# A layer's diagonal state recurrence, from 64 serial complex steps to real scans in a turning frame

## The chip, the cores and the metric

One core of one Trainium2 chip runs the whole program as a single launch. Times are device microseconds of that core, from executions of the compiled kernel; the profile is one execution, recorded by the hardware profiler. Engines are named as in the profile: PE (matmul), DVE (vector), ACT (scalar), POOL (GpSimd), SP (which issues most loads).

## The reference, cut to what matters

The program is one step of a two-layer hybrid encoder. The change touches the S5 branch of layer 0: 32 groups (G) of 64 complex states, each driven by 16 channels.

```python
mag = jnp.exp(lam_re * dt)
ab_re = mag * jnp.cos(lam_im * dt)
ab_im = mag * jnp.sin(lam_im * dt)
...
bu_re = jnp.einsum('btgc,gpc->btgp', ug, bb_re)
bu_im = jnp.einsum('btgc,gpc->btgp', ug, bb_im)
...
_, _, h_re, h_im = lax.associative_scan(_cplx_combine, (a_re, a_im, bu_re, bu_im), axis=1)
y = (jnp.einsum('btgp,gcp->btgc', h_re, c_re) - jnp.einsum('btgp,gcp->btgc', h_im, c_im))
...
y = jax.nn.gelu(y)
y = y * jax.nn.sigmoid(y @ w_glu + b_glu)
```

So h[t] = a·h[t−1] + bu[t] with one complex a per group and state, over a prompt of 16 meta and 2048 frames, and over eight streams of 16 frames.

## The kernel before, in words

Matmuls are made of three products (`mm3`, L111 to L113): operands are split in a high and a low part ("h" and "l": `split`, L105 casts the high part on ACT, L106 subtracts on DVE or POOL).

Every engine runs its instructions in the order of its queue. A planner of the tile framework sets that order when the program is built, by its own estimate of times, within the dependences and the reuse of memory; a tile that takes over another's memory waits until that one's last reader is done. Pools on the "right" side stack on each other.

`phase_in0` normalizes the frames in six blocks (`norm`, `seq`) and multiplies each by the first 1024 columns of the input weights (tiles pm0). The results for the S5 branch stay in `uas` until the end, when ACT copies them out in 32 transfers to `d_ua` (L291). Between the blocks come steps for later phases: at i == 1 `s5_open` (L555) computes the S5 coefficients in many small DVE operations, from λ and dt to the powers of a (`pw`, 17 of them), a16 and bp. At i == 4 the first weight tile of layer 0 is loaded and split ahead: wfh by ACT, wfl by DVE.

`phase_l0` then runs the tiles of the remaining input projection through `mtile`: three passes ("thirds") over pairs of blocks, PE tiles `pm`, a causal convolution on DVE (L537, L539), an ACT SiLU (L408) and the gate matmul L414 (`pg`) that takes its result. After every tile from the third on, `next(s5g, None)` (L496) lets the generator `s5` put out one more step. Its steps are:
- for q in 0..7, four groups each: load u (`s5_u`), the input coefficients `ba` on DVE (L690 to L694), transposes, and the matmul that gives each chunk of 16 frames its contribution, written to `ee` (129 columns a group, two halves: real parts on partitions 0 to 63, imaginary on 64 to 127);
- the scan over chunks: `advance` merges the columns by two (L751 to L755, one operation on POOL), then 64 steps of five DVE operations over all 32 groups (L764 to L768) go along the even columns, and `advance` fills in the odd ones;
- for q in 0..7 the y part: coefficients `ca` (one product on POOL, L818) and matmuls that give y, stored to `d_ys`;
- the end ("s5g"): 32 loads of y (L867) into the place that the y part's pools had, GELU on ACT (L878), and the gated product on PE.

Of the kernel before, what the change touches and what calls it, by code (L numbers as in the profile page):

```python
# [9 lines left out]
F32 = mybir.dt.float32  # L10
# [9 lines left out]
NSEQ = 8  # L20
# [17 lines left out]
def P(e, name, bufs=1, side=None):  # L38
    return e.tc.tile_pool(name=name, bufs=bufs, side=side, reuse_waits="tile")
# [163 lines left out]
def phase_in0(e):  # L203
# [6 lines left out]
    with P(e, "a_w") as wp, P(e, "a_sb", 2) as sb, PS(e, "a_ps") as ps:  # L210
# [37 lines left out]
        for i, bi in enumerate(seq):  # L248
# [306 lines left out]
def s5_open(e, ps):  # L555
# [4 lines left out]
    kb = opn(e, "s5kb", side="right")  # L560
    with P(e, "s5prm", side="right") as sb:
# [37 lines left out]
        pw = s5.pw = keep.tile([128, 2, G, 17], F32, name="s5pw")  # L599
# [4 lines left out]
        t1 = sb.tile([128, G, 16], F32, name="s5t1")  # L604
        t2 = sb.tile([128, G, 16], F32, name="s5t2")
        k = 1
        while k < 16:
# [48 lines left out]
        for q in range(2):  # L656
            hr = sb.tile([128, 128], F32, name=f"s5hr{q}")
            for j, nm in enumerate(("re", "im")):
                src = e.i["state_s5_" + nm].rearrange("a s g p -> (a s g) p")[128 * q:128 * (q + 1)]
                nc.sync.dma_start(hr[:, 64 * j:64 * (j + 1)], src)  # L660
            nc.tensor.transpose(ph[:, q, :], hr, e.ident)
        for q in range(2):
            v.tensor_copy(s5.h0.rearrange("p g (q s) -> p q s g", q=2)[:, q],
                          ph.rearrange("p q (s g) -> p q s g", s=4)[:, q])

# [10 lines left out]
def s5(e, ps):  # L676
# [6 lines left out]
    with P(e, "s5a", side="right") as sb:  # L683
        for q in range(8):
            gs = slice(4 * q, 4 * q + 4)
            ur = s5_u(e, sb, q)
# [8 lines left out]
            v.tensor_copy(p.bb[:, gs, :], ba[:, :, 15, :])  # L695
            bat = sb.tile([128, 4, 2, 128], F32, name="s5bat")
# [17 lines left out]
        v.memset(ee[:, :, 0:1], 0.0)  # L714

        st = sb.tile([128, G, NSEQ], F32, name="s5st")
        s2 = sb.tile([128, G, NSEQ], F32, name="s5s2")
# [5 lines left out]
        sg = sb.tile([128, NSEQ, G], F32, name="s5sg")  # L723
# [9 lines left out]
        yield  # L733

        a32 = sb.tile([128, 2, G], F32, name="s5a32")
        a1 = sb.tile([128, G], F32, name="s5c1", bufs=2)
        a2 = sb.tile([128, G], F32, name="s5c2", bufs=2)
        v.tensor_mul(a1, p.a16[:, 0], p.a16[:, 0])
        v.tensor_mul(a2, p.a16[:, 1], p.a16[:, 1])
        v.tensor_sub(a32[:, 0], a1, a2)  # L740
        v.scalar_tensor_tensor(a32[:, 1], p.a16[:, 0], 2.0, p.a16[:, 1], op0=OP.mult, op1=OP.mult)

        def advance(dst, src, n, g0):

            gs = slice(g0, g0 + G // 2)
            h = ee[:, gs, src:src + 2 * n - 1:2]
            d = ee[:, gs, dst:dst + 2 * n - 1:2]
            t1 = sb.tile([128, G // 2, n], F32, name="s5ba")
            t2 = sb.tile([128, G // 2, n], F32, name="s5tm")
            bc = lambda j, ph: p.a16[ph, j, gs, None].to_broadcast([h[ph].shape[0], G // 2, n])  # L750
            v.tensor_tensor(t2[UP], h[LO], bc(1, LO), op=OP.mult)  # L751
            v.tensor_tensor(t2[LO], h[UP], bc(1, UP), op=OP.mult)
            nc.gpsimd.tensor_tensor(t1, h, bc(0, slice(0, 128)), op=OP.mult)
            v.tensor_add(d, d, t2)
            v.tensor_add(d, d, t1)  # L755

        for g0 in (0, G // 2):
            advance(2, 1, PCH // 2, g0)
            yield
        for c in range(2, PCH + 1, 2):  # L760
            a1 = sb.tile([128, G], F32, name="s5c1", bufs=2)
            a2 = sb.tile([128, G], F32, name="s5c2", bufs=2)
            h = ee[:, :, c - 2]
            v.tensor_tensor(a2[UP], h[LO], a32[LO, 1], op=OP.mult)  # L764
            v.tensor_tensor(a2[LO], h[UP], a32[UP, 1], op=OP.mult)
            v.tensor_tensor(a1, h, a32[:, 0], op=OP.mult)
            v.tensor_add(a2, a2, ee[:, :, c])
            v.tensor_add(ee[:, :, c], a1, a2)  # L768
            if c % 32 == 0:
                yield  # L770
        for g0 in (0, G // 2):
            advance(1, 0, PCH // 2 + 1, g0)
            yield
# [9 lines left out]
    cls(e, "s5kb")  # L783
    with P(e, "s5y", side="right") as sb:

        pw = p.pw
        cp = sb.tile([128, 2, G, 17], F32, name="s5cp")
        v.tensor_copy(cp[UP, 0], pw[UP, 0])
        v.tensor_scalar(cp[LO, 0], pw[LO, 1], -1.0, None, op0=OP.mult)
        v.tensor_scalar(cp[UP, 1], pw[UP, 1], -1.0, None, op0=OP.mult)  # L790
        v.tensor_scalar(cp[LO, 1], pw[LO, 0], -1.0, None, op0=OP.mult)
        cc = [sb.tile([128, G, 16], F32, name=f"s5c{j}") for j in range(2)]
        for j, nm in enumerate(("re", "im")):
            cr = sb.tile([128, 4, 2, 64], F32, name="s5tm2")
# [15 lines left out]
        for q in range(8):  # L810
            gs = slice(4 * q, 4 * q + 4)
            ur = s5_u(e, sb, q)
# [3 lines left out]
            v.tensor_tensor(ca, cp[:, 0, gs, :, None].to_broadcast(sh), cc[0][:, gs, None, :].to_broadcast(sh),  # L816
                            op=OP.mult)
            nc.gpsimd.tensor_tensor(tmp, cp[:, 1, gs, :, None].to_broadcast(sh), cc[1][:, gs, None, :].to_broadcast(sh),  # L818
                                    op=OP.mult)
# [12 lines left out]
            for k in range(8):  # L832
                nc.sync.dma_start(tz[16 * k:16 * (k + 1)],
                                  e.kp[q].rearrange("(g c) a b -> c g a b", g=4)[:16, :, 7 - k:23 - k, :])
            for mh in range(2):
# [18 lines left out]
    cls(e, "s5ee", "s5keep")  # L854
# [1201 lines left out]
```

## Time and profile before

| | before |
|---|---|
| median of 3 runs | 3155.74 us (3153.85 to 3159.35) |
| profiled execution, its span | 3151.14 us, 3149.4 us |
| mean granted TensorE clock | 0.98 |
| PE busy | 3002.9 us (95%), 17435 matmuls |
| weight loads (PEld) busy | 2717.0 us (86%) |
| DVE busy | 1728.6 us (55%) |
| ACT, POOL busy | 1056.1 us (34%), 904.6 us (29%) |
| chain that ended last | PE 59%, DVE 8%, DMA 2% |

A share is an average over all stages. Busy PE is not PE at its full clock: the granted clock stands beside it in the views by stretch. A row of the timeline gives start, duration, engine, line, operation and tiles; in brackets stands the idle time before it and what ended it. "ACTq" and "SPq" rows are the issue of transfers by these engines. A view by groups puts the instructions of one line and shape together: count, busy time, mean nanoseconds, idle time before them.

### The profile page before, as it was taken

The page shows a single profiled execution, that of the slowest core. Times are in us where ns is not written, and L with a number is a line of the kernel's source. Part 1 is how long each engine was busy: PE and PEld are TensorE (multiplying, and loading weights), DVE is VectorE, ACT ScalarE, POOL GpSimd, SP SyncE. Part 2 cuts the span into 40 slices and gives each one's busy share as a digit, 9 for nine tenths or more (in the row PEclk, how much of TensorE's full clock was granted, in tenths as well). Part 3 has the DMA queues.
Part 4 walks back from the last instruction along what each step waited for, and adds up shares of the span by engine and source line. Part 5 has one row for each costly group of instructions (what it writes and reads, how often), then busy time and mean ns, then how long its engine had stood idle before and what let it go on. Part 6 is the DMA issues. An engine that isn't in the chain of part 4 may idle for free.

```text
span 3149.4 us, 45106 instructions
## 1 busy us (share of the span) xinstructions
PE 3002.9 (95%) x17435; PEld 2717.0 (86%) x17435; DVE 1728.6 (55%) x3449; ACT 1056.1 (34%) x1858; POOL 904.6 (29%) x931
## 2 busy tenths in 40 slices
PE   8999978997999998999999999999999999999999
PEld 8999877996987887766799999999998897888887
DVE  4236798464447886243355667766620026665664
ACT  4223332335334443211224555555531112211211
POOL 6104424443225663111202111111110014433432
PEclk9999989998999999999999999999999999999999
DMA  6437433559454556755532111111122158444442
GB/s 213 117 82 206 125 117 113 159 166 177 141 159 125 157 156 183 232 185 172 158 132 73 51 51 50 49 50 49 49 81 75 55 151 251 140 119 133 136 124 74
DMA packets 444034, 396.36 MB, mean 126 GB/s; under 512 B 43401, under 2 KB 392785, under 8 KB 443818
## 3 DMA queue, kind: packets, MB, share of 16 engines
q1 hardware_dynamic: 333164, 268.13, 29.9%
q10 hardware_dynamic: 110654, 125.33, 12.0%
q8 instruction: 137, 2.24, 0.3%
q14 instruction: 79, 0.65, 0.1%
HBM read 262.12 MB, written 131.27 MB: 125 GB/s over the span
## 4 chain that ended last, share of the span: by engine, by line
PE 59%; DVE 8%; DMA 2%; issue 1%; ACT 1%; POOL 0%; SPq 0%; DVEq 0%; POOLq 0%; ACTq 0%
PE p_pm L112 8%; PE p_pm L113 8%; PE p_pm L111 8%; PE r_pm L112 4%; PE r_pm L113 4%; PE r_pm L111 4%; PE pa L111 3%; PE pa L112 3%; PE pa L113 3%; DVE p_d L1639 1%; PE pn L1288 1%; PE pc L1291 1%; DVE p_xc L537 1%; PE pa L1156 1%; DVE m_qs L1131 1%
## 5 line engine op out<-in xcount | busy, mean ns | idle before, releaser
L111 PE MATMUL p_pm<-pu,p_wh 128*128 128x384 f32 (+1 forms) x1568 | 512.2, 327 | 0.2 <-ACT pu L105 0.2
L112 PE MATMUL p_pm<-pu,p_wh 128*128 128x384 f32 (+1 forms) x1568 | 511.9, 327 | 0.0
L113 PE MATMUL p_pm<-pu,p_wl 128*128 128x384 f32 (+1 forms) x1568 | 511.3, 326 | 0.0
L111 PE MATMUL pm<-ub,wh 128*128 128x384 f32 (+1 forms) x1136 | 381.4, 336 | 3.4 <-ACT wh L105 2.9
L112 PE MATMUL pm<-ub,wh 128*128 128x384 f32 (+1 forms) x1136 | 380.1, 335 | 1.6 <-DVE ub L106 1.6
L113 PE MATMUL pm<-ub,wl 128*128 128x384 f32 (+1 forms) x1136 | 376.1, 334 | 0.0
L111 PEld LDWEIGHTS p_pm<-pu,p_wh 128*128 128x128 f32 x1568 | 294.2, 188 | 1.8 <-issue 1.2
L112 PEld LDWEIGHTS p_pm<-pu,p_wh 128*128 128x128 f32 x1568 | 294.6, 188 | 1.0 <-issue 0.8
L113 PEld LDWEIGHTS p_pm<-pu,p_wl 128*128 128x128 f32 x1568 | 294.5, 188 | 0.0
L111 PEld LDWEIGHTS pm<-ub,wh 128*128 128x128 f32 x1136 | 218.6, 193 | 9.0 <-issue 4.3
L112 PEld LDWEIGHTS pm<-ub,wh 128*128 128x128 f32 x1136 | 218.7, 193 | 3.0 <-DVE ub L106 2.1
L112 PE MATMUL r_pm<-rol,r_gh 128*128 128x512 f32 x544 | 217.6, 400 | 3.8 <-POOL rol L106 3.6
L113 PEld LDWEIGHTS pm<-ub,wl 128*128 128x128 f32 x1136 | 218.1, 192 | 1.2 <-issue 1.1
L111 PE MATMUL r_pm<-roh,r_gh 128*128 128x512 f32 x544 | 217.5, 400 | 0.9 <-ACT p_o L1549 0.9
L113 PE MATMUL r_pm<-roh,r_gl 128*128 128x512 f32 x544 | 216.9, 400 | 0.9 <-DVE r_gl L106 0.9
L106 POOL TENSOR_TENSOR p_wl<-p_wr,p_wh 128x1024 fp32r<-128x1024 f32 x34 | 81.8, 2407 | 385.3 <-ACT p_wh L105 372.9
L106 POOL TENSOR_TENSOR wl<-wr,wh 128x1024 fp32r<-128x1024 f32 x47 | 119.2, 2537 | 243.1 <-ACT wh L105 236.8
L112 PEld LDWEIGHTS r_pm<-rol,r_gh 128*128 128x128 f32 x544 | 102.7, 189 | 24.3 <-POOL rol L106 4.1
L113 PEld LDWEIGHTS r_pm<-roh,r_gl 128*128 128x128 f32 x544 | 102.8, 189 | 22.6 <-DVE r_gl L106 1.3
L111 PEld LDWEIGHTS r_pm<-roh,r_gh 128*128 128x128 f32 x544 | 102.3, 188 | 21.9 <-ACT p_o L1549 1.3
L106 POOL TENSOR_TENSOR p_xcl<-p_xc,p_xch 128x384 fp32r<-128x384 f32 (+1 forms) x48 | 46.8, 975 | 245.9 <-ACT p_xch L105 209.3
L1639 DVE RECIPROCAL p_d<-p_d 128x384 f32<-128x384 f32 (+1 forms) x48 | 116.7, 2430 | 0.6
(715 smaller groups left out, 6810.9 us busy)
## 6 DMA issues: line engine op xcount, KB each, us to landing
wr<-in_ev_w_in_dram SPq DMA_DIRECT2D x47, 512.0 KB
p_wr<-in_od_w_in_dram SPq DMA_DIRECT2D x40, 512.0 KB
d_in<-p_o ACTq DMA_DIRECT2D x80, 192.0 KB
m_rw<-d_grow SPq DMA_DIRECT2D x18, 512.0 KB
s5u<-d_ua SPq DMA_DIRECT2D x32, 274.0 KB
d_v<-vo ACTq DMA_DIRECT2D x68, 128.0 KB
m_va<-d_v SPq DMA_DIRECT2D x17, 512.0 KB
d_h<-o_x ACTq DMA_DIRECT2D x17, 512.0 KB
```

The source lines that it names most:

```text
L106: (nc.gpsimd if pool else nc.vector).tensor_tensor(l, x, h, op=OP.subtract)
L111: nc.tensor.matmul(out, a[0], b[0], start=start, stop=False, **kw)
L112: nc.tensor.matmul(out, a[0], b[1], start=False, stop=False, **kw)
L113: nc.tensor.matmul(out, a[1], b[0], start=False, stop=stop, **kw)
L537: v.tensor_scalar(out, x(3), pc[:, m, cw + 3:cw + 4], pc[:, m, cb:cb + 1], op0=OP.mult, op1=OP.add)
L1131: v.tensor_tensor(qs[:, 4 * j:4 * j + 4, :n].rearrange("p (h m) n -> p h m n", m=2), qt[j][:, :, cs].rearrange("p (h m) n -> p h m n", m=2 ...
L1156: nc.tensor.matmul(pS[:n, h, :n], ktc[:, 2 * h + k, :], qt[h // 2][:, 2 * (h % 2) + k, cs], start=k == 0, stop=k == 1)
L1288: nc.tensor.matmul(pn[:n], c.qs[:, 2 * h + k, :n], ct[h][:, k, :], start=False, stop=k == 1)
L1291: nc.tensor.matmul(pc, c.kw[:n, h, 128 * k:128 * (k + 1)], c.va[:n, h, :], start=True, stop=True)
L1639: v.reciprocal(d[:, :n], d[:, :n])
```

## The change

The complex recurrence over the chunks is h[c] = a16·h[c−1] + e[c], a16 = m·exp(iφ). In a frame that turns with it, g[c] = exp(−iφc)·h[c], it becomes g[c] = m·g[c−1] + exp(−iφc)·e[c]: real and imaginary part run apart, with a real coefficient. So the columns of `ee` are turned, four real scans run along them for four groups, and the columns are turned back. The phasors exp(iφc) for c = 0..127 come from seven squarings-up (`s5_phasors`, inside `s5_open`, with four squarings before them) and a table that doubles from column to column (`s5_turns`, still in block i == 1 of the code, four groups of eight, one buffer, 1 MB each, written by ACT's queue to `d_rot`). Each q loads its 512 KB of the table in the layer and scans its own four groups. The serial steps and `advance` are gone, and eight steps fewer stand before the y part. There the product moves from POOL to DVE, and the coefficients cp are made for each q. The powers `pw` move to another pool, and temporaries of `s5_open` are halved.

```diff
                 s5_open(e, ps)
+                s5_turns(e)
+                cls(e, "s5pp")
...
+def s5_phasors(v, sb, pool, s5, cs, sn, mag, keep):
...
+    def square(oc, os_, c, s):
+        v.tensor_mul(t1, c, c)
+        v.tensor_mul(t2, s, s)
+        v.scalar_tensor_tensor(os_, c, 2.0, s, op0=OP.mult, op1=OP.mult)
+        v.tensor_sub(oc, t1, t2)
...
+        v.tensor_mul(oc, oc, t1)
+        v.tensor_mul(os_, os_, t1)
+
+    for _ in range(4):
+        square(c, s, c, s)
+    for j in range(1, ROT):
+        square(pp[:, 0, j], pp[:, 1, j], pp[:, 0, j - 1], pp[:, 1, j - 1])
+
+def s5_turns(e):
...
+    with P(e, "s5co", side="right") as sb:
+        for g0 in range(0, G, 8):
+            gs = slice(g0, g0 + 8)
+            tb = sb.tile([128, 2, 8, 128], F32, name="s5tb")
...
+            v.tensor_copy(tb[:, :, :, 0], p.pp[:, :, 0, gs])
+            for j in range(ROT):
+                k = 1 << j
+                for o in range(0, k, 32):
+                    n = min(k, 32)
...
+                    cmul(v, tb[:, 0, :, k + o:k + o + n], tb[:, 1, :, k + o:k + o + n],
+                         (tb[:, 0, :, o:o + n], tb[:, 1, :, o:o + n]), pk, t1[:, :, :n], t2[:, :, :n])
+            nc.scalar.dma_start(e.rot[:, :, gs, :], tb)
...
-        for q in range(8):
+        def loaded(q):
...
+            rt = sb.tile([128, 2, 4, 128], F32, name="s5rt")
+            nc.sync.dma_start(rt, e.rot[:, :, gs, :])
...
+        def scan(q, rt):
+            gs = slice(4 * q, 4 * q + 4)
+            h = ee[:, gs, 2:PCH + 1]
+            for turn in (v.tensor_sub, v.tensor_add):
+                t1, t2 = halves()
+                v.tensor_tensor(t2[UP], h[LO], rt[LO, 1], op=OP.mult)
+                v.tensor_tensor(t2[LO], h[UP], rt[UP, 1], op=OP.mult)
+                v.tensor_tensor(t1, h, rt[:, 0], op=OP.mult)
+                turn(h, t1, t2)
+                if turn == v.tensor_sub:
+                    for g in range(4 * q, 4 * q + 4):
+                        d = ee[:, g, 1:PCH + 1]
+                        v.tensor_tensor_scan(d, p.m16[:, g:g + 1].to_broadcast([128, PCH]), d, 0.0, op0=OP.mult,
+                                             op1=OP.add)
...
             yield
+            scan(q, rt)
...
-        for g0 in (0, G // 2):
-            advance(2, 1, PCH // 2, g0)
-            yield
-        for c in range(2, PCH + 1, 2):
...
-            v.tensor_tensor(a2[UP], h[LO], a32[LO, 1], op=OP.mult)
-            v.tensor_tensor(a2[LO], h[UP], a32[UP, 1], op=OP.mult)
-            v.tensor_tensor(a1, h, a32[:, 0], op=OP.mult)
-            v.tensor_add(a2, a2, ee[:, :, c])
-            v.tensor_add(ee[:, :, c], a1, a2)
-            if c % 32 == 0:
-                yield
...
-            nc.gpsimd.tensor_tensor(tmp, cp[:, 1, gs, :, None].to_broadcast(sh), cc[1][:, gs, None, :].to_broadcast(sh),
-                                    op=OP.mult)
+            v.tensor_tensor(tmp, cp[:, 1, :, :, None].to_broadcast(sh), cc[1][:, gs, None, :].to_broadcast(sh),
+                            op=OP.mult)
```

The planner lays the orders anew. Three places matter below. A number behind a name tells tiles of one name apart, and "waits" lists the semaphores that a row stands for (DMAHW: a transfer).

ACT, end of the first in-projection. Before, the cast of wfh (the first weights of layer 0) stands among those of the norm (`ub`):

```order
L105 CAST ub_1781<-nrm_t 128x4x128 [waits PE_49]
L218 COPY uas_115<-pm_1846 128x16x17 [waits PE_49]
L105 CAST ub_1781<-nrm_t 128x4x128 [waits PE_49] x2
L105 CAST wfh<-xt 128x1024 [waits DMAHW6_49,DMAHW5_49,DVE_49]
L218 COPY uas_116<-pm_1872 128x16x17 [waits PE_49]
```

After, it stands behind the last two transfers of the table, and the first evictions of layer 0 (`xb`) behind it:

```order
L105 CAST ub_3896<-ut_3897 128x8x128 [waits DMAHW1_49]
L727 DMA d_rot<-s5tb 256x1x1024 [waits DVE_49]
L105 CAST ub_3896<-ut_3901 128x8x128 [waits DMAHW2_49]
L105 CAST ub_3896<-ut_3905 128x8x128 [waits DMAHW3_49]
L727 DMA d_rot<-s5tb 256x1x1024 [waits DMAHW4_49,DVE_49]
L105 CAST wfh<-xt 128x1024 [waits DMAHW6_49,DMAHW4_49]
L386 COPY xb_2664<-pm_2665 128x272 [waits PE_49]
```

The cast now waits for two transfers, its own load and, by its DMAHW4, the one in the row before it. The second transfer of the table stands farther up, behind the 32 issues of `d_ua`.

DVE, at the change from the third group of the table to the fourth (L718 is the first copy of a group, L550 the last operation of one):

```order
L550 TENSOR_TENSOR s5tb<-s5r_1446,s5r_1447 128x8x32 [waits DVE_49]
L106 TENSOR_TENSOR ub_3896<-ut_3897,ub_3896 128x8x128 [waits DMAHW1_49,PE_49,Activation_49]
L106 TENSOR_TENSOR ub_3896<-ut_3901,ub_3896 128x8x128 [waits DMAHW2_49,Activation_49]
L106 TENSOR_TENSOR ub_3896<-ut_3905,ub_3896 128x8x128 [waits DMAHW3_49,Activation_49]
L718 COPY s5tb<-s5pp 128x16 [waits DMAHW6_49,DVE_49]
L545 TENSOR_TENSOR s5r_1499<-s5tb,s5pp 128x8 [waits DVE_49]
```

Nothing of this stood there before. Each group's first copy waits for a transfer: the one that carries the group before it away.

PE, last rows of the first in-projection and first rows of layer 0, before:

```order
L111 MATMUL pm0_2247<-ub1_1781,wh07_106 128x384
L112 MATMUL pm0_2247<-ub1_1781,wh07_106 128x384
L113 MATMUL pm0_2247<-ub1_1781,wl07_114 128x384
L111 MATMUL pm1_2327<-ub0_1507,wfh_2060 128x272
L112 MATMUL pm1_2327<-ub0_1507,wfh_2060 128x272
L113 MATMUL pm1_2327<-ub0_1507,wfl_2061 128x272
```

and after:

```order
L111 MATMUL pm0_2585<-ub1_2119,wh07_107 128x384
L112 MATMUL pm0_2585<-ub1_2119,wh07_107 128x384
L113 MATMUL pm0_2585<-ub1_2119,wl07_115 128x384
L111 MATMUL pm1_2665<-ub0_1845,wfh_2398 128x272
L112 MATMUL pm1_2665<-ub0_1845,wfh_2398 128x272
L111 MATMUL pm1_2691<-ub1_2119,wfh_2398 128x384
L112 MATMUL pm1_2691<-ub1_2119,wfh_2398 128x384
L111 MATMUL pm1_2738<-ub0_1845,wh1_2733 128x272
```

The first tile of layer 0 still takes wfh directly behind the last tile of the in-projection; its third products, with wfl, have moved behind 18 matmuls of another tile.

## Rows read from the trace of the kernel before

**Rows 1.** Windows: busy us (instructions) by engine, PE's clock, DMA share, GB/s

```profile
200.00:250.00 50.00, 50.00 (x326) 50.00 (x325) 0.24 (x2) 6.20 (x14) 0.33 (x3) 1.00 0.52 114
253.30:263.60 10.30, 7.36 (x32) 6.72 (x32) 8.14 (x11) 5.62 (x7) 7.81 (x4) 0.67 1.11 323
350.00:520.00 170.00, 133.02 (x811) 127.22 (x810) 157.89 (x390) 51.06 (x93) 65.73 (x51) 0.88 0.34 105
550.00:600.00 50.00, 50.00 (x345) 48.13 (x344) 21.88 (x20) 17.50 (x33) 19.74 (x15) 1.00 0.59 178
745.00:800.00 55.00, 35.15 (x199) 32.53 (x199) 16.06 (x25) 30.61 (x46) 16.36 (x23) 0.75 0.91 155
```

**Rows 2.** Groups by line, PE, 350:520: busy us, mean ns, idle before

```profile
L111 PE MATMUL pm<-ub,wh 128*128 128x384 f32 x156 | 54.2, 347 | 0.4 <-ACT vo L439 0.4
...
L111 PE MATMUL pm<-ub,wh 128*128 128x272 f32 x48 | 14.5, 302 | 0.0
...
L111 PE MATMUL pm<-wvh,xbh 128*128 128x264 f32 x32 | 10.7, 336 | 1.5 <-ACT xc L382 1.5
```

**Rows 3.** Timeline, PE, end of the first in-projection: start us, us

```profile
243.71 0.33 PE L111 MATMUL pm<-ub,wh 128*128 128x384 f32 x1
...
246.13 0.34 PE L113 MATMUL pm<-ub,wl 128*128 128x384 f32 x1
246.31 0.29 PE L111 MATMUL pm<-ub,wfh 128*128 128x272 f32 x1
...
248.95 0.29 PE L111 MATMUL pm<-ub,wfh 128*128 128x272 f32 x1
```

**Rows 4.** Waits of PE, 240:560: us, times, longest

```profile
PE pg L414 <- ACT xc L408: 26.6, 7, 6.7
PE s5p L778 <- DVE s5fin L775: 8.6, 1, 8.6
```

**Rows 5.** Groups by line, DVE, 350:520

```profile
L768 DVE TENSOR_TENSOR s5ee<-s5c,s5c 128x32 f32<-128x32 f32 x64 | 21.8, 341 | 1.9
...
L764 DVE TENSOR_TENSOR s5c<-s5ee,s5a 64x32 f32<-64x32 f32 x63 | 18.4, 293 | 2.1
...
L754 DVE TENSOR_TENSOR s5ee<-s5ee,s5tm 128x1024 f32<-128x1024 f32 x2 | 6.3, 3134 | 0.0
```

**Rows 6.** Groups by line, DVE, whole span

```profile
L1656 DVE TENSOR_TENSOR_SCAN p_h<-p_d,p_th 128x128 f32<-128x128 f32 x8 | 3.4, 425 | 0.3
```

**Rows 7.** Timeline, DVE, S5 parameters and the last subtraction

```profile
171.06 0.22 DVE L543 TENSOR_TENSOR s5t<-s5pw 128x32 f32<-128x32 f32 x1
...
172.32 0.23 DVE L543 TENSOR_TENSOR s5t<-s5pw 128x64 f32<-128x64 f32 x1
...
175.35 0.42 DVE L543 TENSOR_TENSOR s5t<-s5pw 128x256 f32<-128x256 f32 x1
...
177.86 0.22 DVE L617 TENSOR_TENSOR s5t<-s5lam 128x32 f32<-128x32 f32 x1
...
196.33 1.29 DVE L106 TENSOR_TENSOR ub<-nrm_t,ub 128x512 fp32r<-128x512 f32 x2 [0.19 <-ACT ub L105]
```

**Rows 8.** Waits of DVE, 140:255

```profile
DVE xd L401 <- DMA bif<-in_ml_b_if_dram: 51.3, 1, 51.3
```

**Rows 9.** Timeline, ACT and SP with their queues, 190:260

```profile
193.83 1.05 ACT L105 CAST wfh<-xt 128x1024 fp32r<-128x1024 f32 x1 [1.36 <-DMA xt<-in_ev_w_in_dram]
...
244.55 0.58 ACTq L291 DMA_DIRECT2D d_ua<-uas  x1
...
254.66 1.05 ACT L105 CAST wh<-wr 128x1024 fp32r<-128x1024 f32 x1 [4.75 <-DMA wr<-in_ev_w_in_dram]
...
248.10 1.89 SPq L366 DMA_DIRECT2D wr<-in_ev_w_in_dram  x2
```

**Rows 10.** Waits of PE, and timeline of SP's queue, 735:805

```profile
PE pm L111 <- ACT vo L439: 7.6, 1, 7.6
...
735.06 38.22 SPq L867 DMA_DIRECT2D s5gy<-d_ys  x32
```

More of the change, by code (lines that the diff above doesn't have):

```diff
@@ L560, in s5_open @@
     kb = opn(e, "s5kb", side="right")
+    pool = opn(e, "s5pp", side="right")
     with P(e, "s5prm", side="right") as sb:
@@ L598, in s5_open @@
         nc.scalar.activation(csn, csn, AF.Sin)
-        pw = s5.pw = keep.tile([128, 2, G, 17], F32, name="s5pw")
+        s5_phasors(v, sb, pool, s5, csn, sn, mag, keep)
+        pw = s5.pw = kb.tile([128, 2, G, 17], F32, name="s5pw")
         v.memset(pw[:, 0, :, 0:1], 1.0)
@@ L603, in s5_open @@
         v.tensor_mul(pw[:, 1, :, 1], mag, sn)
-        t1 = sb.tile([128, G, 16], F32, name="s5t1")
-        t2 = sb.tile([128, G, 16], F32, name="s5t2")
+        t1 = sb.tile([128, G, 8], F32, name="s5t1")
+        t2 = sb.tile([128, G, 8], F32, name="s5t2")
         k = 1
@@ L656, in s5_open @@
         for q in range(2):
-            hr = sb.tile([128, 128], F32, name=f"s5hr{q}")
+            hr = sb.tile([128, 128], F32, name="s5hr", bufs=1)
             for j, nm in enumerate(("re", "im")):
@@ L695, in s5, with halves @@
             v.tensor_copy(p.bb[:, gs, :], ba[:, :, 15, :])
+            return ur, ba, rt
+        def halves():
+            t = sb.tile([128, 4, 16, 16], F32, name="s5tm").rearrange("p (x a) b c -> p x (a b c)", x=2)
+            return [t[:, x].rearrange("p (a b) -> p a b", a=4) for x in range(2)]
+        def scan(q, rt):
[12 more added lines that the diff above has]
+                                             op1=OP.add)
+        for q in range(8):
+            ur, ba, rt = loaded(q)
             bat = sb.tile([128, 4, 2, 128], F32, name="s5bat")
@@ L713, in s5 @@
             yield
-        v.memset(ee[:, :, 0:1], 0.0)
-        st = sb.tile([128, G, NSEQ], F32, name="s5st")
-        s2 = sb.tile([128, G, NSEQ], F32, name="s5s2")
+            scan(q, rt)
+        st, s2 = (t[:, 0:2].rearrange("p a (g s) -> p (a g) s", s=NSEQ) for t in halves())
         sh = [64, G, NSEQ]
@@ L722, in s5 @@
         v.tensor_add(st, st, s2)
-        sg = sb.tile([128, NSEQ, G], F32, name="s5sg")
+        sg = sb.tile([128, 4, 2, 128], F32, name="s5bat")[:, 0].rearrange("p a (s g) -> p (a s) g", g=G)
         v.tensor_tensor(sg.rearrange("p s g -> p g s"), st, ed, op=OP.add)
@@ L782, in s5 @@
             nc.scalar.dma_start(e.o["p_s5_" + nm].rearrange("a b g p -> (a b g) p"), so[:, 64 * j:64 * (j + 1)])
-    cls(e, "s5kb")
+    yield
     with P(e, "s5y", side="right") as sb:
[L786 to L792, printed above, removed]
+        pw, cc = p.pw, p.b
         for j, nm in enumerate(("re", "im")):
-            cr = sb.tile([128, 4, 2, 64], F32, name="s5tm2")
+            cr = sb.tile([128, 4, 17, 16], F32, name="s5tm2").rearrange("p a b c -> p (a b c)")
+            cr = cr[:, :512].rearrange("p (a b c) -> p a b c", a=4, b=2)
             for q in range(2):
@@ L809, in s5, with toeplitz @@
                             d16[js, :, None].to_broadcast([16, 8, 16]), op=OP.mult)
-        for q in range(8):
+        def toeplitz(q):
+            ur = s5_u(e, sb, q)
             gs = slice(4 * q, 4 * q + 4)
-            ur = s5_u(e, sb, q)
+            cp = sb.tile([128, 2, 4, 17], F32, name="s5cp")
+            v.tensor_copy(cp[UP, 0], pw[UP, 0, gs])
+            v.tensor_scalar(cp[LO, 0], pw[LO, 1, gs], -1.0, None, op0=OP.mult)
+            v.tensor_scalar(cp[UP, 1], pw[UP, 1, gs], -1.0, None, op0=OP.mult)
+            v.tensor_scalar(cp[LO, 1], pw[LO, 0, gs], -1.0, None, op0=OP.mult)
             ca = sb.tile([128, 4, 17, 16], F32, name="s5ca")
@@ L834, in s5 @@
                                   e.kp[q].rearrange("(g c) a b -> c g a b", g=4)[:16, :, 7 - k:23 - k, :])
+            return ur, ca, tz
+        for q in range(8):
+            ur, ca, tz = toeplitz(q)
             for mh in range(2):
@@ L853, in s5 @@
             yield
-    cls(e, "s5ee", "s5keep")
+    cls(e, "s5ee", "s5kb", "s5keep")
     while not p.loaded:
@@ L1943, in scratch @@
     e.kp = dram.tile([8, 128, 23, 16], F32, name="d_kp")
+    e.rot = dram.tile([128, 2, G, 128], F32, name="d_rot")
     e.u = dram.tile([128, KD, T], F32, name="d_u")
```

60 lines of the change are left out of this document (29 added, 31 removed).

## The prediction

> **What bounds the kernel now.** I read the clock and span first (one core, mean clock 0.98), then the busy shares, then the stretches of layer 0, then its waits, and last the orders of the queues around the change. The span is 3149.4 us, the profiled execution 3151.14 us, and the median of three runs is 3155.74 us; so the profile stands 4.6 us below the median. The sum below is made on the profile and carried to the median by adding its difference. PE is busy 95% of the span: nothing counts unless PE waits less, or more.
>
> The stretches [rows 1] show two things. From 200 to 250 us PE is busy all the time and DVE works 0.24 us: this is free room on DVE. From 350 to 520 us PE is busy 133.02 us of 170, at a granted clock of 0.88, while DVE is busy 157.89. This is the stretch of the old scan. I size PE's loss in it by its matmuls [rows 2]: triples of 384 columns follow each other every 173 ns at the full clock (14 steps from 243.71 to 246.13) and those of 272 every 126 ns (21 steps from 246.31 to 248.95) [rows 3]. So 468 of 384 columns (three lines like the first, 156 each) are 81.0 us, 144 of 272 are 18.1, 108 of 264 at an estimated 122 ns are 13.2, and the other 91, all small, about 9: 121 to 122 us of work in 170. **PE loses about 48 us there**, 37 as idle time and 11 to the lower clock. The waits [rows 4] name the cause: the gate matmul L414 waits for the convolved block (26.6 us in 7 waits), which comes from the DVE operations L537 and L539, and these stand in DVE's queue behind scan steps; and L778 waits 8.6 us for the end of the scan.
>
> **Part one: the scan goes.** Five instructions of 64 steps leave DVE [rows 5]: the first and the dearest are 18.4 and 21.8 us, the five together 90.7 us in this view, and the four "advance" calls some 30 us more (L754 alone took 3.1 us apiece for 128x1024). What comes is, for each of eight q, a turn there and back of 128x512 (two products on half the partitions, one full, one sum) and four real scans of 128x129. A scan of 128x128 takes 425 ns [rows 6]. An operation of 128x256 takes 0.42 us [rows 7], so one of 512 about 0.7 and a half one 0.4 to 0.7, which makes a turn about 2.6, two of them 5.2, the scans 1.7, the coefficients before them (three of 128x1024 at 1.21 us, twice the 512) 3.8, and the convolution of the same time 3.4: 14 us of DVE for each q. In the changed order a q stands every two tiles of PE, that is every 18 us of PE's work. So DVE is filled to three quarters where it was filled to 93%, and no block ahead of a convolution is longer than some 7 us. I keep 6 us of the 48 as small waits (bounds: none, and 20 if each q still holds a convolution back by 2.5 us). **Gain 42.** The product that goes from POOL to DVE in the y part (eight of 128x1088, about 1.3 us each) lies beside a DVE that is busy 21.88 us of 50 there [rows 1], and costs nothing; without that cover it would be 10 us. The 28 further small copies of its coefficients, 0.2 us each as the small ones above, go the same way.
>
> **Part two: the table is made.** The phasors are ten squarings of ten small operations. They go between the norm's subtractions and after them. Six operations of 32 elements, most of them waiting for one another, take 1.26 us (171.06 to 172.32) [rows 7], so the ten of a squaring about 2; one and a piece of them come after the last subtraction (196.33 + 1.3), and the table begins at about 200. A group of the table is one copy and eight complex products. Six operations of 256 elements take 2.5 us (175.35 to 177.86) [rows 7]: three at up to 32 elements (1.26 each), two between them and 256 (an estimate of 3.0 for both) and three of 256 make 14.3 us. Four groups are 57 us. If that was all, they would be done at about 257, mostly in the free room, which DVE spends in one wait of 51.35 us until 248.97 [rows 8].
>
> It is not all. Three things in the orders shown above join the groups to PE. The table has **one buffer**, so each group's first copy waits until the transfer of the group before has landed. The transfers are issued **by ACT, in its order**: the second stands behind the 32 issues of d_ua, the last of which goes out at 244.55 [rows 9]. And **the first weights of layer 0 (wfh) take the table's place**: ACT's cast of wfh, at 193.83 before [rows 9], now waits for the fourth transfer, and PE's first tile of layer 0, at 246.31 before [rows 3], stands behind it in PE's order with nothing between.
>
> The chain, then: group 0 from 200 to 214, landed by 220; group 1 to 234; its transfer issued only at about 246, landed at about 255; group 2 to 270; landed 276; group 3 to 290; landed 296; the cast 1.05 us [rows 9], PE goes on at about 297. A transfer of 1 MB is not in the trace. Two loads of 512 KB, issued from 248.10 on, let the cast behind them begin at 254.66 [rows 9], 6.6 us for the first in a crowd of 311 to 323 GB/s [rows 1]; at that rate 1 MB is 3.2 us of moving. Bounds are 4 and 13 us (twice the crowded one); I take 6 in quiet and 9 for the second, which goes out in the crowd. **PE waits 246.3 to 297, 51 us.** Bounds: 43 with all transfers at 4 us, 60 with the second at 13 and the others at 8. Of this, what PE loses today from 253.3 to 263.6 (32 matmuls in 10.3 us at a clock of 0.67 [rows 1], some 6 us) comes back, since by then all weights lie there; PE starts again at the low clock, which I put at 3 us, half of that loss (bounds 0 and 6). **Cost 48.**
>
> Weighed against this is a rule of the Trainium skill, DMA: Bandwidth & Descriptors, section "Issuing engines are not separate DMA queues": transfers that ACT and SP start run on the same 16 engines and interleave. By that rule the second transfer shares the rate with the loads that SP issues from 248.10 on [rows 9]; an estimate by it is a landing some 7 us later than I take, and a sum of 7 us more. The order in which ACT lets it go, ahead of most of these loads, is why I stay with 9.
>
> **Part three: the gated end of S5.** From 745 to 800 us PE is busy 35.15 us of 55 at a clock of 0.75 [rows 1]: 199 matmuls at 126 to 173 ns are 25 to 34 us, so 21 to 30 are lost. PE waits 7.6 us for ACT's vo in one wait [rows 10], and ACT stands in a GELU whose 32 loads SP issues from 735.06 for 38.22 us [rows 10]. In the new order the S5 steps end earlier against the tiles, and about 5 us more of PE's work lie between the last of them and the gated products. I take 5 us of gain (bounds 0 and 10).
>
> **The sum:** −42 + 48 − 5 = +1. Against the profile's 3151.1 that is 3152, against the median **3157 us**.
>
> **Rivals.**
> *Faster, by about 16 us (3140 us).* The transfers land in 4 to 5 us and the groups overlap as drawn, the wait is 43 to 45 us; two thirds of the small waits vanish; the end gains 9: 44 − 3 − 46 − 9 = −14 to −18. For it: DVE has nothing else from 250 on. Against it: operations of 3.1 us [rows 5] show that DVE is slowed when POOL works. It is decided by the landing time: with 2 us less in each of three landings PE gains 6.
> *Slower, by about 22 us (3178 us).* The second transfer, behind d_ua on ACT and beside SP's loads, lands at 262 or later and the others at 8 us: the wait is 60 us instead of 51, the small waits are 13 instead of 6, the end gains nothing: 60 − 3 − 35 + 0 = +22. The point is where PE takes its first matmul of layer 0: from 303 us on this is the case. The rule of the skill named above speaks for it.
> *The table does not hold PE (3118 us).* If wfh had its own place, or the cast did not wait for the fourth transfer, the table would end in DVE's free room and PE lose 10 to 15 us at most: 12 − 3 − 42 − 5 = −38. The order speaks against it: the cast carries the wait.
>
> **How the numbers follow.** Faster or slower means by over 0.2%, 6.3 us, about what a measurement of this kernel can tell from no change. My forecast of no difference has 0.36. The faster rival has 0.27 and the table that does not hold PE 0.05: 0.32 in all. The slower rival has 0.32. These hold much the same weight because two sums of nearly 50 us, each uncertain by 6 to 10, are taken from each other. The range leaves out the last rival and the far ends of the others: 3136 to 3182. The likeliest case alone reaches from 3150 to 3163.
>
> **What would show it.** Right: PE idle from about 246 to 297 us with the first wfh matmul behind it, waiting for ACT's cast, and that for the fourth d_rot transfer; four groups of 14 us on DVE with gaps at 214, 234 and 270; the gate matmul's waits down from 26.6 us to a few; the same PE work in the scan's stretch in 48 us less, but for 6. Wrong: PE's first wfh matmul before 285 or after 305; waits of L414 above 15 us; or a stretch of GELU that loses as much as before.

## The result, and the profile after

| | before | after |
|---|---|---|
| median of 5 runs each | 3153.85 us (3149.38 to 3159.35) | 3174.29 us (3168.98 to 3178.73) |
| ratio | 1 | 1.007, 95% interval 1.0055 to 1.0084 |
| profiled execution, its span | 3151.14 us, 3149.4 us | 3178.73 us, 3176.3 us |
| mean granted TensorE clock | 0.980 | 0.974 |

The change makes the kernel 0.7% slower, some 20 us. That lies inside the range, but not in the case forecast as likeliest (no difference); the slower rival's 3178 us came nearer, though not by its mechanism. The profiled executions stand 28 us apart (their spans 27), because the one of before is 3 us under its median and the one of after 4 us over its own.

By stretch, the columns as in [rows 1]:

```profile
250.00:300.00 50.00, 5.82 (x35) 5.82 (x36) 36.64 (x105) 6.70 (x7) 6.24 (x5) 0.53 0.65 201
310.00:525.00 215.00, 193.19 (x1292) 186.12 (x1294) 172.84 (x200) 81.54 (x162) 81.10 (x65) 0.94 0.47 142
550.00:600.00 50.00, 48.78 (x340) 46.12 (x339) 28.52 (x30) 19.21 (x36) 17.59 (x15) 1.00 0.59 180
750.00:800.00 50.00, 36.48 (x213) 33.82 (x212) 26.64 (x39) 29.90 (x43) 25.74 (x28) 0.80 0.99 185
```

The free room of DVE is used (25.50 us of 50 from 200 on in another row of this view, 36.64 of 50 from 250 on), and in the second of these stretches PE has nearly nothing to do, 5.82 us. The granted clock of 0.53 there is nearly the lower of its two levels, 1.2 GHz, and stands for a stretch in which PE was idle but for its end. The steps with the scan, 310 to 525, still leave PE idle 22 us of 215, at 0.94. PE's waits from 200 to 900 us:

```profile
PE pm L111 <- ACT wfh L105: 48.1, 1, 48.1
PE s5p L793 <- DVE s5ba L761: 14.4, 4, 3.8
PE pm L111 <- ACT xb L386: 9.9, 3, 4.7
PE pg L416 <- ACT xc L410: 5.8, 3, 3.0
...
PE s5p L818 <- DVE s5bat L815: 3.6, 1, 3.6
```

One wait is new and long, that for wfh. The wait of the gate matmul is down from 26.6 us [rows 4] to 5.8, and that for the end of the scan from 8.6 to 3.6 (now the transposes L818). In their place PE's transposes of the input coefficients (L793) wait four times, 14.4 us. The chain of the first wait, in the timeline (the four first copies of the table's groups on DVE; the last d_ua issue, three d_rot issues and the cast on ACT; PE's first tile of layer 0):

```profile
199.90 0.19 DVE L718 COPY s5tb<-s5pp 128x16 f32<-128x16 f32 x1
...
219.21 0.18 DVE L718 COPY s5tb<-s5pp 128x16 f32<-128x16 f32 x1 [5.35 <-DMA d_rot<-s5tb]
...
250.61 0.18 DVE L718 COPY s5tb<-s5pp 128x16 f32<-128x16 f32 x1 [17.55 <-DMA d_rot<-s5tb]
...
274.88 0.18 DVE L718 COPY s5tb<-s5pp 128x16 f32<-128x16 f32 x1 [1.04 <-DMA d_rot<-s5tb]
...
243.89 0.53 ACTq L293 DMA_DIRECT2D d_ua<-uas  x1
244.51 0.97 ACTq L727 DMA_DIRECT2D d_rot<-s5tb  x1
...
269.84 0.52 ACTq L727 DMA_DIRECT2D d_rot<-s5tb  x1
...
288.76 0.52 ACTq L727 DMA_DIRECT2D d_rot<-s5tb  x1
293.08 1.04 ACT L105 CAST wfh<-xt 128x1024 fp32r<-128x1024 f32 x1 [20.70 <-DMA d_rot<-s5tb]
...
294.18 0.60 PE L111 MATMUL pm<-ub,wfh 128*128 128x272 f32 x1 [48.06 <-ACT wfh L105]
```

I read PE's loss in a stretch as before: its length less its matmuls at the full-clock intervals.

| stage | loss before | loss after |
|---|---|---|
| end of the in-projection, first weights (before 246 to 264, after 246 to 310) | 6.0 | 49.2 |
| first part of the layer, inputs and scan (264 to 520; 310 to 525) | 52.9 | 35.5 |
| y part (520 to 745; 525 to 750) | 11.7 | 11.1 |
| gated end (745 to 850; 750 to 850) | 31.1 | 23.1 |

The sum is +17 us, of the 27 between the two spans. Some 7 of the rest lie behind 850 us, by the same reading, spread over the later stages; no single wait there was traced.

Why do the steps with the scan still lose 35 us, when DVE is busy no more than 172.84 of 215 us? The operations in this stretch, by groups:

```profile
L777 DVE TENSOR_TENSOR s5tm<-s5ee,s5rt 64x512 f32<-64x512 f32 x16 | 17.3, 1081 | 0.2
...
L761 DVE TENSOR_TENSOR s5ba<-s5ba,s5tm 128x1024 f32<-128x1024 f32 x8 | 16.3, 2034 | 0.2
...
L783 DVE TENSOR_TENSOR_SCAN s5ee<-s5m,s5ee 128x129 f32<-128x129 f32 x32 | 12.2, 441 | 0.2
...
L539 DVE TENSOR_SCALAR xc<-xb,pc 128x656 f32<-128x656 f32 x8 | 12.4, 1546 | 6.8 <-ACT xb L386 6.8
```

An L777 is 64x512 and takes 0.69 us when it runs alone, an L761 of 128x1024 1.22 us; their means are 1.08 and 2.03. The timeline tells when. Here are two of POOL's subtractions of a weight tile, three DVE operations beside them, and the PE transpose behind:

```profile
357.34 2.69 POOL L106 TENSOR_TENSOR wl<-wr,wh 128x1024 fp32r<-128x1024 f32 x1 [7.02 <-ACT wh L105]
...
363.25 2.34 POOL L106 TENSOR_TENSOR wl<-wr,wh 128x1024 fp32r<-128x1024 f32 x1 [3.19 <-ACT wh L105]
...
357.08 0.69 DVE L776 TENSOR_TENSOR s5tm<-s5ee,s5rt 64x512 f32<-64x512 f32 x1
357.78 2.79 DVE L777 TENSOR_TENSOR s5tm<-s5ee,s5rt 64x512 f32<-64x512 f32 x1
...
363.29 3.38 DVE L761 TENSOR_TENSOR s5ba<-s5ba,s5tm 128x1024 f32<-128x1024 f32 x1
...
366.82 0.45 PE L793 MATMUL s5p<-ident,s5ba 128*128 128x128 f32 x1 [3.85 <-DVE s5ba L761]
```

L776 starts before POOL does and takes 0.69 us. L777, alike in size, starts 0.4 us after POOL's subtraction and ends at 360.57, half a microsecond after it (360.03). L761 starts with the next one and ends at 366.67, a microsecond after it (365.59). PE's transpose of what L761 writes waits 3.85 us, nearly what the two lost (2.1 and 2.2 us). The Trainium skill, GPSIMD Engine Reference, section "1. Specifications", says that POOL's SBUF interfaces are shared with VectorE, with contention for DVE instructions with two SBUF inputs or in a 2-port mode. The trace agrees, and gives the size: such an operation does not merely run slower, it ends nearly its own length (0.55 of 0.69 us, 1.08 of 1.22) behind POOL's end.

### The profile page after: what moved, and what is told of

It reads as the page before. It is cut to its first block, busy times and chain, and to the rows that moved or that the text cites. A ratio compares the mean times of both kernels' runs of the same rounds, so it can differ in the third digit from the quotient of the medians.

```text
span 3176.3 us, 45217 instructions
## 1 busy us (share of the span) xinstructions
PE 3005.6 (95%) x17435; PEld 2718.8 (86%) x17435; DVE 1776.8 (56%) x3550; ACT 1059.1 (33%) x1860; POOL 879.2 (28%) x919
## 4 chain that ended last, share of the span: by engine, by line
PE 60%; DVE 8%; DMA 2%; issue 1%; ACT 1%; POOL 0%; DVEq 0%; POOLq 0%; ACTq 0%; SPq 0%
PE p_pm L112 8%; PE p_pm L113 8%; PE p_pm L111 8%; PE r_pm L113 4%; PE r_pm L111 4%; PE r_pm L112 4%; PE pa L111 3%; PE pa L112 3%; PE pa L113 3%; DVE p_d L1695 1%; PE pc L1347 1%; PE pn L1344 1%; PE pa L1212 1%; DVE m_qs L1187 1%; PE r_o L1897 1%
```

## The experiments

Two theories were to be told apart for each of the two losses. For the wait: the table's place under wfh and its chain of transfers, against a DVE that is late anyhow. For the scan's stretch: DVE operations held by POOL, against a DVE that is short of time as a whole. All medians are of runs beside runs of the kernel before on the same chip, and the ratios are against those; the changed kernel's own is 1.007, and differences to it go by the ratios.

**1. First weights by the ordinary path.**

```diff
-            if i == 4:
-                fp = opn(e, "w_first", side="right")
...
-                split(nc, *e.wf, wr)
...
-        if (third, m, isz) == (0, 0, 0):
-            wh, wl = e.wf
-        else:
+        if True:
             wr = sb.tile([128, KD, 128], F32, name="wr1")
```

> The changed kernel, but the first weight tile of layer 0 is no longer loaded and split ahead: it goes the way of all others, in memory of its own. Theory A (PE's 48 us wait comes from wfh taking the place of the table): the wait for wfh is gone, PE begins layer 0 when ordinary weights land, at about 257 us instead of 294, and stops once more for some 5 to 10 us, because ACT's evictions stand behind the third transfer of the table in ACT's order. 25 to 35 us less: 3140 to 3149 us. Rival B (the four groups hold PE anyhow, by DVE's and ACT's order): PE's first tile ends its waits at 285 or later, and the time falls by less than 8 us.

Measured: 3154.78 us, ratio 1.0017 (1.0005 to 1.0029), some 17 us under the changed kernel. PE's waits from 200 to 530:

```profile
PE s5p L782 <- DVE s5ba L750: 16.3, 4, 5.2
PE pm L111 <- ACT wh L105: 10.2, 2, 9.7
PE pg L407 <- ACT xc L401: 7.8, 3, 4.0
```

The wait of 48.1 us is gone; PE begins layer 0 after 9.7 us, at 255.75. So it was the table's place. But less came back than the 25 to 35 us expected: from 270 to 310 PE loses 13 us (it waits 6.3 us for the gate's convolution, which DVE does beside the groups, and 1.9 us for POOL's wl), and L782, the transposes, wait 16.3 us.

**2. The transfers on SP's queue.**

```diff
-            nc.scalar.dma_start(e.rot[:, :, gs, :], tb)
+            nc.sync.dma_start(e.rot[:, :, gs, :], tb)
```

> The changed kernel, but the table's four transfers are issued by SP instead of ACT. Theory A (the second transfer is late because it stands behind 32 issues of d_ua on ACT): it goes out at 234 instead of 244.5, DVE's wait of 17.5 us before the third group falls to 5 or 6, PE goes on at about 281 instead of 294: 3161 us. Rival B (the transfers share the 16 engines with d_ua, so the queue does not matter): the second transfer lands after 246, the gain is under 5 us.

Measured: 3168.83 us, ratio 1.0058 (1.0037 to 1.0078), not told apart from the changed kernel. The two first issues on SP, the third group on DVE, and a wait of SP's queue from 200 to 300:

```profile
214.30 27.99 SPq L727 DMA_DIRECT2D d_rot<-s5tb  x2
...
249.42 0.18 DVE L718 COPY s5tb<-s5pp 128x16 f32<-128x16 f32 x1 [16.08 <-DMA d_rot<-s5tb]
```

```profile
SPq L727 <- DMA d_ua<-uas: 26.8, 1, 26.8
```

Rival B's signs hold: the second issue ends at 242.3, though group 1 was done on DVE at 233.3, and the transfer lands after 246, since the third group begins at 249.42. But its reason, a share of the 16 engines, is not shown: the view puts this wait of SP's queue, 26.8 us, down to a transfer of d_ua, which ACT issued, so the issue itself was held before anything of it moved. Why an issue on SP's queue waits for that transfer stays open. The run so says nothing for or against the rule of the Trainium skill, DMA: Bandwidth & Descriptors, section "Issuing engines are not separate DMA queues", that the prediction weighed.

**3. One group of the table.**

```diff
-        for g0 in range(0, G, 8):
+        for g0 in range(0, 8, 8):
...
-            nc.sync.dma_start(rt, e.rot[:, :, gs, :])
+            nc.sync.dma_start(rt, e.rot[:, :, 4 * (q % 2):4 * (q % 2) + 4, :])
```

> The changed kernel with only the first of the table's four groups made and stored; all eight q load their turns from it, so the states of the other groups are turned by wrong angles. This leaves out three quarters of the table and keeps all else. Theory A (the stall is the chain of groups, the scan's own gain is 17 us plus 8 at the gated end): the wait for wfh is gone, PE begins layer 0 at 246, time 3130 us, 24 us under the kernel before. Rival B (the scan's gain is the 42 us of the prediction and was eaten by something that the table does later): 3107 us or less.

Measured: 3127.02 us, ratio 0.9928 (0.9905 to 0.995). Theory A, within 3 us. The wait for wfh is gone and PE loses 1.5 us from 246 to 264. So the last three groups cost 45 us, all of what the change loses and more, and the rest of the change, with the gated end, is worth 22 us, not 47.

**4. The scan behind the next inputs.**

```diff
             yield
-            scan(q, rt)
...
+            if q:
+                scan(q - 1, rt)
+            rt = turned(q)
+            yield
+        scan(7, rt)
```

(`turned` loads the q's part of the table, which `loaded` did.)

> The changed kernel, but each q's scan is put out after the coefficients, transposes and matmuls of the next q, not before them; the table's part for q is loaded after the scan of the one before. Same instructions. Theory A (DVE's input coefficients stand behind the scan, which POOL stretches beyond the planner's times, and PE's transposes L793 wait for them, 14.4 us and as much again by the low clock): these waits fall under 4 us, the time by 15 to 25 us: 3150 to 3159. Rival B (DVE as a whole is short of time there): the waits go to the gate matmul and the transposes at the end, the time moves by less than 6 us.

Measured: 3174.11 us, ratio 1.0082 (1.0055 to 1.011): nothing. PE's waits from 300 to 900:

```profile
PE pg L416 <- ACT xc L410: 12.4, 7, 3.8
PE s5p L796 <- DVE s5ba L759: 8.9, 4, 5.2
PE s5p L113 <- DVE ut L106: 7.7, 1, 7.7
```

My theory A falls in this form. The transposes still wait (L796, 8.9 us), the gate matmul more (12.4), and a wait of 7.7 us appears in the gated end. The waits moved more than they went, as rival B has it; number 5 tells against its cause. How the planner laid DVE's order here was not traced.

**5. The weight tiles' low part on DVE.**

```diff
-            split(nc, wh, wl, wr, pool=True)
+            split(nc, wh, wl, wr, pool=False)
```

> The changed kernel, but the low part of layer 0's weight tiles is subtracted on DVE (128x1024, about 1.25 us) instead of POOL (about 2.4 us). Theory A (a DVE operation that meets POOL's subtraction is held until that ends, some 2.1 us on one operation for each weight tile, and PE's transposes wait for what is held): the long forms of L776 to L778 and L761 vanish (L777 from 1081 ns mean to 700, L761 from 2034 to 1220), the waits of L793 on L761 fall from 14.4 us to under 6, and the time falls by 8 to 20 us although DVE has more to do: about 3158 us. Rival B (DVE is short of time as a whole, and 1.25 us more for each tile makes it worse): the waits move to PE's wait for wl or the gate matmul, and the time stays within 5 us or rises.

Measured: 3142.75 us, ratio 0.9976 (0.9966 to 0.9985): some 30 us under the changed kernel, where 8 to 20 were expected, and faster than the one before. Its stretch 310 to 525, and its DVE groups from 290 on:

```profile
310.00:525.00 215.00, 210.95 (x1467) 204.40 (x1466) 178.87 (x242) 90.02 (x179) 43.23 (x57) 0.99 0.52 159
```

```profile
L106 DVE TENSOR_TENSOR wl<-wr,wh 128x1024 fp32r<-128x1024 f32 x20 | 24.7, 1235 | 22.3 <-ACT wh L105 22.3
...
L777 DVE TENSOR_TENSOR s5tm<-s5ee,s5rt 64x512 f32<-64x512 f32 x16 | 12.0, 751 | 0.2
...
L761 DVE TENSOR_TENSOR s5ba<-s5ba,s5tm 128x1024 f32<-128x1024 f32 x8 | 10.8, 1350 | 0.2
```

DVE has more to do than before this edit (178.87 us against 172.84) and PE is busy 210.95 us against 193.19: PE's loss falls from 35.5 to 8.5 us. L777 is at 751 ns, and the transposes' wait is not among the waits any more. DVE was not short of time; it was late at single operations. What was taken from POOL costs 1.24 us on DVE and takes away 2 us of holding.

**6. Two halves for one buffer.**

```diff
-            tb = sb.tile([128, 2, 8, 128], F32, name="s5tb")
+            tb, hi = [sb.tile([128, 2, 8, 64], F32, name="s5t" + x) for x in "bh"]
...
-            nc.scalar.dma_start(e.rot[:, :, gs, :], tb)
+            nc.scalar.dma_start(e.rot[:, :, gs, 0:64], tb)
+            nc.scalar.dma_start(e.rot[:, :, gs, 64:128], hi)
```

> The changed kernel, but each group of the table lies in two tiles, columns 0 to 63 and 64 to 127, with a transfer of 512 KB each; no more memory. Theory A (one buffer makes each group wait for the transfer of the one before): while one half is carried away the other is computed, so the gaps of 5.4, 17.5 and 1 us before the groups nearly vanish, the last group ends at about 260, wfh is cast at 266, and PE goes on at 267 instead of 294: 25 us less, 3147 us. Rival B (the transfers on ACT's queue stand behind d_ua whatever their size): the third group still begins at 248 or later, PE goes on at 285 or later, under 10 us less.

Measured: 3165.47 us, ratio 1.005 (1.0032 to 1.0067), some 6 us under the changed kernel, in intervals that overlap; PE's wait for wfh is 41.8 us instead of 48.1. First copies of groups 1 to 3 on DVE; on ACT the issue of group 1's first half, that of the last half, and the cast:

```profile
214.00 0.19 DVE L718 COPY s5tb<-s5pp 128x16 f32<-128x16 f32 x1 [0.25 <-DMA d_rot<-s5tb]
...
237.06 0.18 DVE L718 COPY s5tb<-s5pp 128x16 f32<-128x16 f32 x1 [9.22 <-DMA d_rot<-s5tb]
...
255.70 0.18 DVE L718 COPY s5tb<-s5pp 128x16 f32<-128x16 f32 x1
...
231.93 0.95 ACTq L728 DMA_DIRECT2D d_rot<-s5tb  x1
...
277.90 0.59 ACTq L729 DMA_DIRECT2D d_rot<-s5th  x1
286.76 1.04 ACT L105 CAST wfh<-xt 128x1024 fp32r<-128x1024 f32 x1 [13.34 <-DMA d_rot<-s5th]
```

Group 1 follows group 0 at once, but its first half goes out at 231.93 only, among d_ua's issues, so group 2 waits 9.2 us. And the last group takes from 255.70 to 277.9, 22 us instead of 14: three subtractions of 1.22 us stand in it, and POOL's subtractions begin at 262 beside it (three operations of 128x256 in a row, L545 to L547, took 2.61, 2.56 and 1.40 us there, and take 0.42 alone). The edit also changed the transfers themselves: from 195 to 300 us 17376 packets are under 512 bytes, against 928 in the changed kernel, and the last half, 512 KB, took 8.9 us from its issue to the cast, where the last whole group took 4.3. So the run does not tell what two buffers alone would give. It shows that the wait for the one buffer was a part of the loss, not that it was all.

**7. Halves and the ordinary path**, together.

> The two halves, and the first weight tile by the ordinary path (nothing of layer 0 takes the table's place). Theory A: PE begins layer 0 when the ordinary weights land, about 256, and the table, done by about 262, holds only the first convolutions a little: 8 to 12 us less than with the halves alone, 3137 us. Rival B (the first tiles wait for DVE, which is behind with the table): waits of the gate matmul eat it, and the time equals that of the halves alone within 4 us.

Measured: 3149.97 us, ratio 0.9998 (0.9987 to 1.0008): level with the kernel before, and 15 us under the halves alone, more than expected.

**8. All three.**

> The two halves, the ordinary path for the first weights, and the subtraction of layer 0's weight tiles on DVE. If both theories hold, the two gains add: 3125 us, faster than both kernels (some 24 us under the one before). Rival B of the subtraction: no better than the two halves with the ordinary path, 3137 us or more.

Measured: 3117.15 us, ratio 0.9896 (0.9879 to 0.9913). The gains add.

**9. The kernel before, with the weight tiles' low part on DVE.** The edit of 5 on the old scan.

> The kernel before, with the subtraction of layer 0's weight tiles on DVE instead of POOL and nothing else. Theory A (the holds cost in every stretch in which DVE is tight, so also in the old scan): 8 to 20 us less than before, 3131 to 3143 us. Rival B (DVE is full in the old scan, 158 of 170 us, so that 1.25 us more for each tile takes back what the holds give): within 6 us of the kernel before, and the gain needs the real scans.

Measured: 3127.32 us, ratio 0.993 (0.9912 to 0.9948). Theory A, and more than its 8 to 20 us. The old scan too lost much of its time to the holds: PE's loss from 264 to 520 falls from 52.9 to 28.6 us.

**10. Both engines subtract.** The edit of 5, and beside it, for each tile:

```diff
+            for k in (slice(0, 4), slice(4, 8)):
+                idle = sb.tile([128, 4, 128], mybir.dt.bfloat16, name="idle", bufs=1)
+                nc.gpsimd.tensor_tensor(idle, wr[:, k], wh[:, k], op=OP.subtract)
```

> The kernel with the subtraction on DVE, and beside it POOL subtracts the same tiles once more, into a scratch tile that nobody reads (two operations of half the size). DVE's and PE's work is that of the subtraction on DVE alone; nothing waits for POOL's copy but the reuse of the tiles. Theory A (a DVE operation that meets POOL's is held until it ends): the long forms are back, L776 to L778 and L761 show operations of 1.5 to 3 us again, and most of the gain is lost: 3160 to 3180 us. Rival B (the gain came from another order of DVE's queue, or from PE not waiting for POOL's result): the time stays within 6 us of the subtraction on DVE alone, 3143 us.

Measured: 3195.1 us, ratio 1.0139 (1.0117 to 1.0161), 52 us over number 5. DVE groups from 300 to 540 (numbering moved by three lines; L780 is L777 above), and PE's wait for the transposes:

```profile
L782 DVE TENSOR_TENSOR s5ee<-s5tm 128x512 f32<-128x512 f32 x16 | 15.3, 956 | 0.3
L780 DVE TENSOR_TENSOR s5tm<-s5ee,s5rt 64x512 f32<-64x512 f32 x16 | 15.2, 951 | 0.2
...
L764 DVE TENSOR_TENSOR s5ba<-s5ba,s5tm 128x1024 f32<-128x1024 f32 x8 | 11.8, 1469 | 0.2
```

```profile
PE s5p L796 <- DVE s5ba L764: 15.8, 5, 4.9
```

With POOL's operations back, though nobody needs their result, the means go up again (L780 951 ns against 751, L782 956 against 694), the transposes wait 15.8 us and PE loses 36 us from 310 to 540. The copies can reach PE by one other way, the reuse of the tiles: SP's loads of the weights wait 25 us for them in all, but from 300 to 560 PE waits 0.7 us for a weight tile. So it is POOL's running that costs, not PE's waiting for POOL. The order is laid anew here too, and a small part by that is not ruled out. The time is 15 us above the range of theory A. Some of it is the start of the layer, where PE waits 56.5 us for wfh against 51.8 in number 5; the rest was not traced.

**11 and 12. All of POOL's large subtractions of layer 0 on DVE**, in the version of number 8 and in the kernel before.

```diff
-        nc.gpsimd.tensor_tensor(xbl[:, :ncol], xb[:, 3:3 + ncol], xbh[:, :ncol], op=OP.subtract)
+        nc.vector.tensor_tensor(xbl[:, :ncol], xb[:, 3:3 + ncol], xbh[:, :ncol], op=OP.subtract)
...
-        split(nc, wvh, wvl, wv, pool=True)
+        split(nc, wvh, wvl, wv, pool=False)
```

> The best version so far (halves, ordinary path, layer 0's weight subtraction on DVE), with POOL's other large subtractions of layer 0 on DVE too (xbl 128x656 or 128x768, wvl 128x528). Theory A: what POOL holds up is taken from it wherever it moves; 310 to 525 us lost about 13 us there, and 4 to 8 of them come back: 3110 us. Rival B: DVE, busy 170 of 215 us there, is now short of time, and the convolutions come late: 3120 us or more.

> The kernel before with all of these subtractions of layer 0 on DVE: the old serial scan, without POOL's large operations beside it. Theory A: the serial scan still fills DVE, so it gains less than the real scans do from this: 3120 to 3128 us, and the version with the real scans stays 8 us or more ahead. Rival B: the old scan does as well as the new one once POOL is out of its way, within 4 us.

Measured: number 11 3101.41 us, ratio 0.9839 (0.9821 to 0.9857), the fastest of all; number 12 3125.09 us, ratio 0.9915 (0.9898 to 0.9932). The real scans lead by 24 us. But not in the scan. The stretches of 11 and of 12:

```profile
310.00:525.00 215.00, 212.51 (x1471) 205.59 (x1470) 165.97 (x253) 88.68 (x175) 18.27 (x39) 0.99 0.56 168
```

```profile
350.00:520.00 170.00, 163.99 (x1057) 157.74 (x1056) 154.25 (x434) 63.21 (x111) 25.94 (x35) 0.98 0.46 139
```

The old serial scan, without POOL beside it, keeps PE busy 163.99 us of 170, where it was 133.02 [rows 1], though DVE works nearly as long, 154.25 us against 157.89. The lead lies later. PE's waits of number 12 from 200 to 900:

```profile
PE s5p L111 <- ACT ut L105: 19.8, 1, 19.8
PE s5p L971 <- issue: 17.6, 1, 17.6
PE s5p L1038 <- DMA m_va<-in_state_ml_n_dram: 9.3, 1, 9.3
```

In number 12 the gated end of S5 is over at 840 us and layer 0's last tile at 849; the gate chain behind it (L971, L1038) then finds no tile to cover it, and PE waits 17.6 and 9.3 us there. In number 11 the S5 steps, eight fewer, are over at 798 and the tiles at 861, and neither wait is over 0.3 us. These two waits are 27 us, about the lead. But other terms are as large: number 12 also waits 19.8 us for ut in its gated end, and number 11 waits 14.9 us for its first weights, which number 12 has ahead, and idles 16 us from 525 to 750, where number 12 idles 2. So what the lead is made of is argued here and not shown, and that the fewer steps are its cause was not tried by itself.

## Why the prediction was right or wrong

**The wait for wfh: right, in mechanism and size.** PE was to wait from 246.3 to 297, 51 us; it waited 48.1, until 294.18. The groups were to start at 200, 220, 255 and 276 and started at 199.90, 219.21, 250.61 and 274.88. Two errors cancelled, which is luck: the second transfer landed 4 us earlier than I took, and the third group took 19 us instead of 14.3. The second error is the holds again: beside POOL's subtractions, from 256.13 to 262.15, L548 to L550 of 128x128 took 2.33, 2.43 and 1.27 us, and take 0.29 alone. (The estimate by the rule of the Trainium skill, DMA: Bandwidth & Descriptors, section "Issuing engines are not separate DMA queues", a landing 7 us later than I took, was farther off; number 2 shows nothing against the rule itself.) The last transfer took 4.3 us from issue to the cast. PE's restart at the low clock cost 1.3 us, not 3: its matmuls of 128x272 come every 226 ns until 297.0, and every 126 ns from there on. The net cost of this part was 43 us where the sum had 48.

**The scan's gain: right in direction, wrong in size, and this is the step that failed.** "I keep 6 us of the 48 as small waits", with 20 as the outer bound: it was 35.5 us (over 310 to 525; some 22 of it idle, the rest the lower clock), and the gain 17 instead of 42. I reckoned a q by durations of operations that ran alone, 14 us of DVE against 18 of PE, and took a filling of three quarters as enough. The operations beside POOL's were in the rows, L754 with 3.1 us [rows 5], and I named them against the faster rival without pricing them. Numbers 5 and 10 show them to be nearly the whole of the miss: without POOL's subtractions of the weight tiles the stretch loses 8.5 us, near the 6 forecast, and with idle ones PE loses 36 again (over 310 to 540). I also took the old scan's 48 us for the price of a serial scan; with POOL's operations gone it loses some 11 us (number 12).

**The gated end: right.** 5 us of gain were forecast, 8 came.

**The rivals.** The sum was to be +1; by its terms it became 43 − 17 − 1 − 8 = +17 (the 1 is the y part), and the medians say +20. That the time still lies in the range is luck: its upper part was drawn for late transfers, and was filled by a scan 25 us dearer than forecast. The slower rival had the right end with the wrong place: it wanted a wait of 60 us and 13 us of small waits, and it was 48 and 35. The faster one fell on the holds. That the table need not hold PE was shown by number 1, where PE begins layer 0 at 255.75; but the time was 3155 us, not 3118, with the scan's gain at 17 and not 42, and 13 us lost from 270 to 310. With three quarters of the table left out (number 3) it was 3127.

## What to carry to other kernels

Before costing an operation from the trace, look at what ran on the other engine that reads the same memory: two rows of one form that differ by the length of a POOL operation are a hold, and an engine with time to spare can still be late at each point where it matters. Here a subtraction that POOL did in 2.4 us "for nothing" cost DVE 2 us at each meeting, and 1.24 us when DVE did it itself. Whether a hold costs the program anything depends on who waits for the result: from 525 to 750 us DVE's operations are held by some 46 us in all (an estimate: their lengths beside POOL's less those of the same forms alone), and PE loses 11 us there, before the change and after. When work is moved into free room, follow who inherits its memory and who stands behind its transfers in each queue: here 57 us of work in 51 us of room became a wait of 48 us because the next phase's first weights took the buffer's place.

## What the runs showed of the hardware

In these traces a DVE operation with two SBUF inputs that starts while POOL subtracts 128x1024 ends behind POOL's end by little less than its own time alone: 0.55 us for 64x512, which takes 0.69 alone and took 2.79, and 1.08 us for 128x1024, which takes 1.22 and took 3.38. The one that started first goes on: L776, 0.26 us ahead of POOL, took its 0.69, and POOL's subtraction, which began beside it, took 2.69 where the next took 2.34. An operation with one tensor input is hit too: L539 (128x656) has a mean of 1546 ns, and takes 0.62 where nothing runs beside it. A real scan of 128x129 took 441 ns in the mean in the changed kernel, because one of the 32 was held to 1.48 us, and 406 in number 5, against 425 for 128x128 [rows 6], so that price was right.
